# Fewer, larger transfers around the attention of a hybrid encoder layer, and a third bank for the maxima

## The chip, the cores and the metric

The kernel runs on one core of a Trainium2 chip. A core has five engines that work side by side, each with its own queue of instructions: TensorE (PE, with its weight loads as PEld), VectorE (DVE), ScalarE (ACT), GpSimd (POOL) and SyncE (SP), which here issues nearly all transfers. Sixteen DMA engines move the data between the chip's memory (DRAM tiles and tensors) and the on-chip buffers. TensorE writes its products into PSUM, eight banks of 512 fp32 columns for 128 partitions. The metric is the device time of one launch in microseconds.

## The reference

One layer for two groups of requests that share weights: a prompt of 2048 frames, and 8 sample streams of 16 new frames each with 1024 cached ones. Each goes through a combined input projection, then in parallel a causal depthwise convolution and an attention with a learned forgetting bias, then an output projection and a gated feed-forward network. What matters here is the attention:

```
def _attend(q, k, v, cum_q, cum_k, q_pos, k_pos):
    s = jnp.einsum('bqhd,bkhd->bhqk', q, k, preferred_element_type=jnp.float32) * (HEAD_DIM ** -0.5)
    s = s + (cum_q[..., :, None] - cum_k[..., None, :])
    mask = k_pos[None, :] <= q_pos[:, None]
    s = jnp.where(mask, s, NEG_INF)
    p = jax.nn.softmax(s, axis=-1)
    return jnp.einsum('bhqk,bkhd->bqhd', p.astype(v.dtype), v)
```

There are 8 heads of 64 channels; `cum` is the running sum of the log forget values of a head. All data are fp32.

## The kernel before

**Stages.** The trace shows them in this order: the projections of the gated inputs, values and forget values (to about 340 us), those of queries and keys (to about 600 us), the attention (to about 1190 us), the output projection (to about 1400 us), and the feed-forward network (to the end). Only the attention and what feeds it are touched.

**The prompt's attention.** Heads go in 4 pairs p, queries in 4 blocks qb of 512; a step is one (p, qb) of `STEPS`, 16 in all. A softmax needs each query's maximum before the scores can be exponentiated with keys on the partitions, so the scores are made twice. `score_maxima` makes them with queries on the partitions, in pieces of 512 keys: one product `mx` (L952), for the diagonal a mask product (L956), and a VectorE reduction into `M` (L957). A step has 8(qb+1) pieces, 8, 16, 24 or 32. After a step the maxima `Z` are transposed into `pz` (L968), copied to `mrow` (L970) and sent to the row `AUX` of the operand `Q2` of that step (L972), where they enter the second making of the scores as one more row of the contraction. `attend` makes these: `s` from two products (L1035 with `K1` and `Q1`, L1041 with `K2` and `Q2`) and a mask product on the diagonal (L1043), the exponential `e` on ScalarE (L1045), the products with the values `pv` (L999), and the sums of `e` by products with ones (L988) and by additions on GpSimd (L1011) and VectorE. Pieces run ahead of the scores: 32 at first (`AHEAD`), later up to 42 by an order written in `attend`.

**The end of a step.** `end_of_step` copies the unnormalised output to `zc`, the sums to `sm` (rows 0, 32, 64, 96), and sends them row by row to `sum_d` (L1080). Some units of work later, by a list of due times, `load` brings them back on 128 partitions (L1084), `invert` adds and inverts them and sends them to `inv_d` (L1090), `back` spreads each head's inverses over 64 partitions of `R` (L1094), and `divide` multiplies (L1097) and stores.

**The background.** `background` is woven between the scores: first the norm of the convolution, then the sample streams. `sample_setup` makes the forgetting bias of all streams and heads and sends it to `bias_d` (four quarters of keys) and `biasn_d` (new keys). `next_bias` loads a stream's bias into `S`, two streams ahead: 8 transfers for four quarters and two heads (L1218), 2 for the new keys (L1222). `sample_scores` adds products to it (lane matmuls, all under the helper's line L1105), `sample_values` takes the softmax and the values. Keys `kc` (L1208) and values `vc` (L1234) of a stream come as two transfers of 1 MB each, with 3 and 2 buffers.

**Order and banks.** The tile framework's planner fixes each engine's order when the kernel is built; some orders are forced by hand (`after`, `late`). The banks are shared out by name: `BANKS = {"u": 3, "cv": 2, "tr": 2, "ss": 1}`. In the attention `u` holds the scores `s`, `cv` the pieces `mx` and the transposes `pz`, `tr` the outputs and sums, `ss` the background's lanes.

Of the kernel before, what the change touches and what calls it, by code (L numbers as in the profile page):

```python
# [6 lines left out]
F32 = mybir.dt.float32  # L7
# [4 lines left out]
ALU = mybir.AluOpType  # L12
# [4 lines left out]
P = 128  # L17
# [3 lines left out]
NTP = T // P  # L21
NT = NTP + 1
TT = NT * P
NS = 8
QS = 16
H = 8
HD = 64
NP = H // 2
PAST = 1024
# [17 lines left out]
AHEAD = 32  # L47
# [11 lines left out]
AUX = 96  # L59


def f32(ap):
    return ap.bitcast(F32)
# [64 lines left out]
class Layer:  # L128
# [30 lines left out]
    def run(self, stop=99):  # L159
        tc = self.tc  # L160
        self.pinned = self.last_load = None
        self.LZ = ExitStack()
        with ExitStack() as ctx:
            d = self.dram = ctx.enter_context(tc.tile_pool(name="dram", bufs=1, space=DRAM))
            self.keep = ctx.enter_context(self.pool(name="keep", bufs=1))
            self.LB = ExitStack()
            self.big = self.LB.enter_context(self.pool(name="big", bufs=16, side="right"))
            self.ps = ctx.enter_context(self.pool(name="ps", bufs=1, space=PSUM))
            self.h_d = d.tile([P, CB, 2, TT], F32, name="h_d")
            self.u_d = d.tile([P, 4, HIST + T], F32, name="u_d")  # L170
            self.y_d = d.tile([P, 4, TT], F32, name="y_d")
            self.q_d = d.tile([H, P, T], F32, name="q_d")
            self.k_d = d.tile([H, P + 2, T], F32, name="k_d")
            self.cat_d = d.tile([P, CB, TT], F32, name="cat_d")
            self.x1_d = d.tile([P, CB, TT], F32, name="x1_d")
            self.ht_d = d.tile([P, 3, 7, 4, NW], F32, name="ht_d")
            self.r_d = d.tile([len(HALVES), P, NW], F32, name="r_d")
            self.gt_d = d.tile([P, 3, 7, NF // 2, NW], F32, name="gt_d")
            self.sup_d = d.tile([NF, 4, P, 512], F32, name="sup_d")
            self.sdn_d = d.tile([3, 4, 4, P, 512], F32, name="sdn_d")  # L180
            self.bias_d = d.tile([4, NS * H, PAST // 4], F32, name="bias_d")
            self.biasn_d = d.tile([NS * H, QS], F32, name="biasn_d")
            self.qs_d = d.tile([P, NP, P], F32, name="qs_d")
            self.sum_d = d.tile([NP, 4, 4, 512], F32, name="sum_d")
            self.inv_d = d.tile([NP, 4, 2, 512], F32, name="inv_d")
            self.open_input()
            self.load_constants()
            with ExitStack() as c1:
                self.project_u_v(c1)
            if stop > 1:  # L190
                self.project_q_k()
            if stop > 2:
                with ExitStack() as c2:
                    self.attention(c2)
                self.out_projection(stop)
                return
            else:
                while self.todo:
                    self.parts(9, TT)
                self.conv_part(999, TT)  # L200
            for st in (self.LZ, self.LC, self.RS, self.R, self.L, self.LB):
                st.close()
# [728 lines left out]
    def score_maxima(self):  # L931

        nc = self.nc
        self.mx, self.nscore, self.last_product = [], 0, None
        spread = None
        for n, (p, qb) in enumerate(STEPS):
            if qb == 0:
                self.loading = self.keys(p)
            self.kv[p] = next(self.loading)
            K2 = self.kv[p][1]  # L940
            Q2, Z, M = self.Q2[n % 4], self.Z[n % 2], self.M[n % 2]
            if n < 2:
                nc.gpsimd.memset(Z, 0.0)
            t = slice(qb * 512, qb * 512 + 512)
            nc.sync.dma_start(f32(Q2[0:HD]), self.q_d[2 * p:2 * p + 2, 0:HD, t].rearrange("h r t -> r h t"))
            for i in range(8):
                h, j = i // 4, i % 4
                for kb in range(qb + 1):
                    diag = kb == qb
                    w = (j + 1) * P if diag else 512  # L950
                    mx = self.bank("cv", "mx")
                    self.mx.append(nc.tensor.matmul(mx[:, :w], Q2[0:AUX, h, j * P:(j + 1) * P], K2[kb][0:AUX, h, :w], start=True, stop=not diag))  # L952
                    if self.last_product:
                        self.after(self.mx[-1], self.last_product)
                    if diag:
                        nc.tensor.matmul(mx[:, w - P:w], self.masks[:, 2], self.masks[:, 0], start=False, stop=True)  # L956
                    self.last_max = nc.vector.tensor_reduce(M[:, i, kb:kb + 1], mx[:, :w], AX.X, ALU.max)  # L957
                    if spread and i * (qb + 1) + kb == 3:
                        self.spread_maxima(*spread)
                    yield 0  # L960
            nc.vector.tensor_reduce(Z[:, AUX:AUX + 8], M[:, :, 0:qb + 1], AX.X, ALU.max)
            spread = (Z, Q2)
        self.spread_maxima(*spread)

    def spread_maxima(self, Z, Q2):
        nc, r = self.nc, slice(AUX, AUX + 8)
        pz = self.bank("cv", "pz", (P, P))
        nc.tensor.transpose(pz, Z, self.ident)  # L968
        m = self.lp.tile([P, P], F32R, tag="mrow", name="mrow", bufs=1)
        nc.vector.tensor_copy(m[r], pz[r])  # L970
        for i in range(8):
            nc.sync.dma_start(f32(Q2[AUX:AUX + 1, i // 4, i % 4 * P:(i % 4 + 1) * P]), f32(m[AUX + i:AUX + i + 1]))  # L972

    def attend(self, p, qb, n):

# [86 lines left out]
    def end_of_step(self, p, qb, zc, sums):  # L1062


        nc, wk = self.nc, self.awk
        parts = 2 if qb else 1
        r = slice(0, 64 * parts)
        sm = wk.tile([P, 512], F32, tag="sm", name="sm", bufs=1)
        self.last_exp = nc.scalar.copy(sm[r], sums[r])
        cat = self.cat_d[:, 4 + p, qb * 512:(qb + 1) * 512]  # L1070
        R = wk.tile([P, 512], F32, tag="R", name="aR", bufs=1)
        if (p, qb) == STEPS[-1]:
            spread = self.bank("ss", "R")
# [2 lines left out]
            nc.vector.tensor_tensor(zc, zc, R, ALU.mult)  # L1076
            nc.gpsimd.dma_start(cat, zc)
            return
        for i in range(2 * parts):
            nc.sync.dma_start(self.sum_d[p, qb, i:i + 1], sm[32 * i:32 * i + 1])  # L1080
        w = wk.tile([P, 2, 2, 4], F32, tag="inv", name="inv")

        def load():
# [6 lines left out]
            nc.sync.dma_start(self.inv_d[p, qb].rearrange("h (a c) -> a h c", c=4), w[:, 0])  # L1090

        def back():
            for h in range(2):
                nc.sync.dma_start(R[HD * h:HD * h + HD], self.inv_d[p, qb, h:h + 1].broadcast_to([HD, 512]))  # L1094

        def divide():
            self.after(nc.vector.tensor_tensor(zc, zc, R, ALU.mult), self.last_max)  # L1097
# [37 lines left out]
    def sample_setup(self, bank):  # L1135

        nc, a, sm = self.nc, self.a, self.smp
# [9 lines left out]
        sel = sm.tile([P, NS + QS], F32, name="sel")  # L1147
# [14 lines left out]
        for h in range(2):  # L1162
            o = slice(HD * h, HD * h + HD)
# [12 lines left out]
        for b in range(2):  # L1176
            pb = bank.rearrange("p (i k) -> p i k", i=4)
            for i in range(4):
# [4 lines left out]
                suf[:n, 4 * b:4 * b + 4].unsqueeze(2).broadcast_to([n, 4, P]), ALU.add)  # L1183
            yield
        lm = sm.tile([P, NS, H], F32, name="lm")
        nc.vector.tensor_tensor(lm, self.logf[:, NTP, :].unsqueeze(1).broadcast_to([P, NS, H]),
                                sel[:, 0:NS].unsqueeze(2).broadcast_to([P, NS, H]), ALU.mult)
        yield
        pn = bank[:, :QS]
        self.pe(pn[:n, :], lm.rearrange("p s h -> p (s h)"), sel[:, NS:], start=True, stop=True)  # L1190
# [20 lines left out]
    def next_bias(self, b):  # L1211

        if b < NS:
            S = self.smp.tile([P, PAST + NP * QS], F32, tag="S", name="S", bufs=2)
            for j in range(4):
                for h in range(2):
                    rows = self.bias_d[j].rearrange("(s g h) k -> s h g k", s=NS, h=2)[b, h]
                    self.nc.sync.dma_start(S[32 * j + QS * h:32 * j + QS * h + QS, :PAST].rearrange("p (g k) -> p g k", g=NP),  # L1218
                                           rows.unsqueeze(0).broadcast_to([QS, NP, PAST // 4]))
            for h in range(2):  # L1220
                rows = self.biasn_d.rearrange("(s g h) k -> s h g k", s=NS, h=2)[b, h]
                self.nc.sync.dma_start(S[QS * h:QS * h + QS, PAST:].rearrange("p (g k) -> p g k", g=NP),  # L1222
                                       rows.unsqueeze(0).broadcast_to([QS, NP, QS]))
            kS = self.smp.tile([P, NP, QS], F32, tag="kS", name="kS", bufs=2)
            self.nc.sync.dma_start(kS, self.a["o_k"][:, :, T + b * QS:T + (b + 1) * QS].rearrange("g p t -> p g t"))
            self.S.append((S, kS))
# [559 lines left out]
def host_layout(inp):  # L1786
    import numpy as np

    inp = {n: np.asarray(v) for n, v in inp.items()}

    def c(x):
        return np.ascontiguousarray(x)
# [5 lines left out]
    def cols(w):  # L1798
# [21 lines left out]
        "w_down": c(inp["w_down"][0].reshape(NF // 2, 2, P, CB, P).transpose(1, 3, 2, 0, 4)),  # L1820
        "kcT": c(inp["cache_k"][0].reshape(NS, PAST, NP, P).transpose(0, 3, 2, 1)),
        "vc": c(inp["cache_v"][0].reshape(NS, PAST, DC)),
        "clfT": c(inp["cache_logf"][0].reshape(NS, 8, P, H).transpose(2, 1, 0, 3).reshape(P, 8, NS * H)),
        "ident": np.eye(P, dtype=np.float32),
    }
    i = np.arange(P)
# [8 lines left out]
    g = i % 32 // 8  # L1835
# [39 lines left out]
```

## Time and profile before

| | us |
|---|---|
| median of 3 runs (2797.84 to 2798.93) | 2798.88 |
| the profiled execution by its own time | 2804.1 |
| its span, first to last instruction | 2802.3 |
| PE busy in the span | 2716.7 (97%) |
| DVE busy | 2029.7 (72%) |
| ACT busy | 1235.4 (44%) |
| share of the 16 DMA engines in use by the hardware queue | 67.0% |

How to read the profile: all durations come from the one profiled execution. The times of windows and timelines count from the span's start. In a timeline row the number in brackets is the time that the engine stood idle before the instruction, with the instruction or transfer that ended the wait. A row of a group of instructions ends with its busy time, the mean duration of one, and the idle time before them. "PEclk" is TensorE's granted clock as a share of full speed. A SyncE row such as `SPq L972 DMA_DIRECT2D Q<-mrow x8` is eight issues of transfers from tile `mrow` to tile `Q`; its duration is the time of the issuing, not of the transfers.

### The profile page before, as it was taken

How to read it: one execution, taken by the hardware profiler on the slowest of the kernel's cores; microseconds unless marked ns; L12 is line 12 of the kernel's file. 1: busy time of each engine (PE TensorE's matmuls, PEld its weight loads, DVE VectorE, ACT ScalarE, POOL GpSimd, SP SyncE). 2: the span in 40 equal slices, each digit the busy share in tenths (PEclk: the TensorE clock that was granted, in tenths of full speed). 3: DMA queues.
4: the chain of work that ended last, by engine and by line, in shares of the span. 5: the costliest groups of instructions: out<-in, count | busy, mean ns of one | idle time of the engine just before them, and what ended most of it. 6: DMA issues, size and time to landing. Idle time of an engine off the chain costs nothing.

```text
span 2802.3 us, 49088 instructions
## 1 busy us (share of the span) xinstructions
PE 2716.7 (97%) x16930; PEld 2397.9 (86%) x16930; DVE 2029.7 (72%) x4132; ACT 1235.4 (44%) x2472; POOL 500.6 (18%) x686
## 2 busy tenths in 40 slices
PE   7999999999999989999999999999999999999999
PEld 6899988874445545498999999999999999999999
DVE  2798898974656566545397989877887778776765
ACT  4543323343444333444354446444554446555552
POOL 3454411223443221314201120000000000000000
PEclk9999999989999999999999999999999999999999
DMA  8863567673436577265576869866786769787873
GB/s 320 255 193 107 177 225 260 207 199 97 131 105 179 160 223 240 62 218 189 172 264 204 303 205 314 275 213 215 243 285 208 227 194 319 248 284 252 278 248 116
DMA packets 416978, 603.55 MB, mean 215 GB/s; under 512 B 65141, under 2 KB 280341, under 8 KB 414681
## 3 DMA queue, kind: packets, MB, share of 16 engines
q1 hardware_dynamic: 416520, 600.05, 67.0%
q8 instruction: 133, 2.18, 0.3%
q14 instruction: 117, 0.95, 0.1%
q0 software_dynamic: 208, 0.37, 0.0%
HBM read 426.00 MB, written 174.25 MB: 214 GB/s over the span
## 4 chain that ended last, share of the span: by engine, by line
PE 82%; DMA 8%; DVE 5%; issue 2%; ACT 1%; POOL 1%; SPq 1%; DVEq 0%; ACTq 0%; POOLq 0%
PE z L1665 45%; PE z L524 6%; PE acc L1353 5%; PE pv L999 4%; PE mx L952 3%; PE pa L332 3%; PE pvv L352 3%; PE pg L332 3%; PE s L1035 2%; PE lane L1105 2%; PE s L1041 2%; PE sm L988 1%; DMA wraw<-w_in 1%; DVE rW L1370 1%; DMA kc<-kcT 1%
## 5 line engine op out<-in xcount | busy, mean ns | idle before, releaser
L1665 PE MATMUL z<-rT,rW 128*128 128x360 f32 (+1 forms) x8316 | 1384.4, 328 | 3.9 <-ACT rW L1369 1.4
L1665 PEld LDWEIGHTS z<-rT,rW 128*128 128x128 f32 x8316 | 1380.1, 188 | 6.3 <-ACT rW L1369 2.4
L1369 ACT ACTIVATE rW<-rR 128x512 fp32r<-128x512 f32 x714 | 434.7, 616 | 388.7 <-PE z L1665 277.0
L1370 DVE TENSOR_TENSOR rW<-rR,rW 128x512 fp32r<-128x512 f32 x714 | 477.3, 673 | 160.3 <-ACT rW L1369 155.8
L712 DVE SCALAR_TENSOR_TENSOR cv<-cu,cpar,cv 128x384 f32<-128x384 f32 x580 | 311.7, 615 | 2.5 <-ACT cv L710 2.4
L1045 ACT ACTIVATE e<-s 128x512 f32<-128x512 f32 (+3 forms) x320 | 166.4, 532 | 284.2 <-PE s L1041 163.9
L957 DVE TENSOR_REDUCE M<-mx 128x1 f32<-128x512 f32 (+2 forms) x320 | 190.2, 605 | 133.7 <-PE mx L952 106.4
L524 PE MATMUL z<-hqx,wqh 128*128 128x384 f32 (+1 forms) x768 | 197.4, 333 | 1.3 <-DVE logf L359 1.3
L1369 ACT ACTIVATE rT<-traw 128x360 fp32r<-128x360 f32 (+1 forms) x315 | 149.8, 501 | 81.8 <-DMA traw<-gt_d 50.8
L1370 DVE TENSOR_TENSOR rT<-traw,rT 128x360 fp32r<-128x360 f32 (+1 forms) x315 | 158.0, 531 | 34.0 <-ACT rT L1369 33.3
L952 PE MATMUL mx<-K,Q 96*128 96x512 f32 (+2 forms) x320 | 142.4, 458 | 21.1 <-DVE M L957 12.6
L999 PE MATMUL pv<-e,V 128*64 128x512 f32 (+3 forms) x640 | 157.1, 558 | 0.0
L952 PEld LDWEIGHTS mx<-K,Q 96*128 96x128 f32 x320 | 62.8, 199 | 109.9 <-DVE M L957 57.2
L524 PEld LDWEIGHTS z<-hqx,wqh 128*128 128x128 f32 x768 | 136.1, 188 | 17.6 <-issue 12.4
L1353 PE MATMUL acc<-ch,woh 128*128 128x360 f32 (+1 forms) x384 | 127.1, 333 | 6.3 <-DVE xo L1361 3.9
L1593 DVE TENSOR_TENSOR rR<-rR 128x512 f32<-128x512 f32 (+1 forms) x136 | 92.0, 696 | 56.6 <-DMA rR<-w_down 50.5
L1035 PE MATMUL s<-Q,K 128*128 128x512 f32 (+3 forms) x320 | 131.0, 409 | 0.3 <-ACT e L1045 0.2
L1353 PE MATMUL acc<-ch,wol 128*128 128x360 f32 (+1 forms) x384 | 126.7, 330 | 0.0
L524 PE MATMUL z<-hqx,wql 128*128 128x384 f32 (+1 forms) x384 | 126.5, 329 | 0.0
L1041 PE MATMUL s<-Q,K 128*128 128x512 f32 (+3 forms) x320 | 120.3, 376 | 4.6 <-DMA Q<-mrow 4.6
L1353 PE MATMUL acc<-cl,woh 128*128 128x360 f32 (+1 forms) x384 | 122.9, 330 | 0.7 <-DVE cl L1370 0.6
L1011 POOL TENSOR_TENSOR sums<-e,sums 128x512 f32<-128x512 f32 x72 | 97.4, 1353 | 100.2 <-ACT e L1045 96.9
(317 smaller groups left out, 3728.5 us busy)
## 6 DMA issues: line engine op xcount, KB each, us to landing
rR<-sup_d SPq DMA_DIRECT2D x176, 256.0 KB
rR<-w_gate SPq DMA_DIRECT2D x132, 256.0 KB
traw<-gt_d SPq DMA_DIRECT2D x154, 180.0 KB
rR<-w_down SPq DMA_DIRECT2D x104, 256.0 KB
rR<-sdn_d SPq DMA_DIRECT2D x96, 256.0 KB
rR<-w_up SPq DMA_DIRECT2D x88, 256.0 KB
sup_d<-rR SPq DMA_DIRECT2D x88, 256.0 KB
wa<-w_ada SPq DMA_DIRECT2D x16, 1024.0 KB
```

The costliest lines, as they stand in the source:

```text
L332: nc.tensor.matmul(pz[:, :n], w[:, m], x[:, :n], start=(c == 0 and k == 0), stop=(c == CB - 1 and k == 2))
L524: nc.tensor.matmul(z[:, :n], w[:, m], x[:, :n], start=(c == 0 and k == 0), stop=(c == CB - 1 and k == 2))
L712: self.pin(nc.vector.scalar_tensor_tensor(dst, src, w, acc[i], ALU.mult, ALU.add))
L952: self.mx.append(nc.tensor.matmul(mx[:, :w], Q2[0:AUX, h, j * P:(j + 1) * P], K2[kb][0:AUX, h, :w], start=True, stop=not diag))
L957: self.last_max = nc.vector.tensor_reduce(M[:, i, kb:kb + 1], mx[:, :w], AX.X, ALU.max)
L999: product = nc.tensor.matmul(z[0][HD * h:HD * h + HD, off:], V[kt // 4][:, kt % 4, HD * h:HD * h + HD], es[h][:, off:], start=(kt == 0), s ...
L1035: first = nc.tensor.matmul(s[:, off:], K1[kb][:, h, sl], Q1[:, h, off:], start=True, stop=False)
L1041: self.last_s = nc.tensor.matmul(s[:, off:], K2[kb][:, h, sl], Q2[:, h, off:], start=False, stop=not diag)
L1353: self.nc.tensor.matmul(z[:, :n], w[:, m], y, start=(first and i == 0 and k == 0), stop=(last and i == len(terms) - 1 and k == 2))
L1369: copy = self.nc.scalar.activation(hi, raw, AF.Copy)
L1370: engine.tensor_tensor(lo, raw, f32(hi), ALU.subtract)
L1665: nc.tensor.matmul(z, W[:, x, m], t[:, y, :w], start=(k == 0 and i == 0), stop=(k == n - 1 and i == 2))
```

## The change

It does five things.

- Sums: a step's rows of `sm` go to `sum_d` in one transfer with a partition step of 32.
- Inverses: both heads go to `R` in one transfer, its source the two rows of `inv_d`, each repeated 64 times.
- Maxima: the eight rows of `mrow` go to a new DRAM tile `mrow_d` in one transfer; `take_maxima` brings them to the row of `Q2` in another, four pieces later.
- Bias: the rows of the forgetting bias are ordered stream, head of the pair, pair (before: stream, pair, head of the pair), from the host's layout of the cached forget values on. So a quarter of a stream's bias is one transfer, its source two rows of 4 KB, each repeated 16 times; the bias of the new keys is a fifth. The product `lm` is made in two halves for this order.
- Banks: from the 42nd piece of maxima on, each third is made in a bank of `u`.

```diff
+            self.mrow_d = d.tile([8, P], F32, name="mrow_d")
...
-                    mx = self.bank("cv", "mx")
+                    mx = self.bank("u" if len(self.mx) > AHEAD + 8 and len(self.mx) % 3 == 2 else "cv", "mx")
...
-                    if spread and i * (qb + 1) + kb == 3:
-                        self.spread_maxima(*spread)
+                    if spread and i * (qb + 1) + kb in (3, 7):
+                        (self.spread_maxima if i * (qb + 1) + kb == 3 else self.take_maxima)(*spread)
...
         self.spread_maxima(*spread)
+        self.take_maxima(*spread)
...
-        for i in range(8):
-            nc.sync.dma_start(f32(Q2[AUX:AUX + 1, i // 4, i % 4 * P:(i % 4 + 1) * P]), f32(m[AUX + i:AUX + i + 1]))
+        nc.sync.dma_start(self.mrow_d, f32(m[r]))
+
+    def take_maxima(self, Z, Q2):
+        self.nc.sync.dma_start(f32(Q2[AUX:AUX + 1]).rearrange("o h q -> o (h q)"), self.mrow_d.rearrange("(o r) c -> o (r c)", o=1))
...
-        for i in range(2 * parts):
-            nc.sync.dma_start(self.sum_d[p, qb, i:i + 1], sm[32 * i:32 * i + 1])
+        nc.sync.dma_start(self.sum_d[p, qb, 0:2 * parts], sm[0:64 * parts:32])
...
-            for h in range(2):
-                nc.sync.dma_start(R[HD * h:HD * h + HD], self.inv_d[p, qb, h:h + 1].broadcast_to([HD, 512]))
+            nc.sync.dma_start(R, self.inv_d[p, qb].unsqueeze(1).broadcast_to([2, HD, 512]))
...
-        nc.vector.tensor_tensor(lm, self.logf[:, NTP, :].unsqueeze(1).broadcast_to([P, NS, H]),
-                                sel[:, 0:NS].unsqueeze(2).broadcast_to([P, NS, H]), ALU.mult)
+        for h in range(2):
+            nc.vector.tensor_tensor(lm[:, :, NP * h:NP * h + NP], self.logf[:, NTP, h::2].unsqueeze(1).broadcast_to([P, NS, NP]),
+                                    sel[:, 0:NS].unsqueeze(2).broadcast_to([P, NS, NP]), ALU.mult)
...
-                for h in range(2):
-                    rows = self.bias_d[j].rearrange("(s g h) k -> s h g k", s=NS, h=2)[b, h]
-                    self.nc.sync.dma_start(S[32 * j + QS * h:32 * j + QS * h + QS, :PAST].rearrange("p (g k) -> p g k", g=NP),
-                                           rows.unsqueeze(0).broadcast_to([QS, NP, PAST // 4]))
-            for h in range(2):
-                rows = self.biasn_d.rearrange("(s g h) k -> s h g k", s=NS, h=2)[b, h]
-                self.nc.sync.dma_start(S[QS * h:QS * h + QS, PAST:].rearrange("p (g k) -> p g k", g=NP),
-                                       rows.unsqueeze(0).broadcast_to([QS, NP, QS]))
+                rows = self.bias_d[j].rearrange("(s h g) k -> s h (g k)", s=NS, h=2)[b]
+                self.nc.sync.dma_start(S[32 * j:32 * j + 32, :PAST], rows.unsqueeze(1).broadcast_to([2, QS, PAST]))
+            rows = self.biasn_d.rearrange("(s h g) k -> s h (g k)", s=NS, h=2)[b]
+            self.nc.sync.dma_start(S[:32, PAST:], rows.unsqueeze(1).broadcast_to([2, QS, NP * QS]))
...
-        "clfT": c(inp["cache_logf"][0].reshape(NS, 8, P, H).transpose(2, 1, 0, 3).reshape(P, 8, NS * H)),
+        "clfT": c(inp["cache_logf"][0].reshape(NS, 8, P, NP, 2).transpose(2, 1, 0, 4, 3).reshape(P, 8, NS * H)),
```

## The prediction

> **What bounds the kernel now.** I read the page's chain of work that ended last first, then the windows of the attention stage, then the timelines of TensorE, VectorE and SyncE around its gaps, and last the DMA view of short stretches.
>
> ```profile
> PE 82%; DMA 8%; DVE 5%; issue 2%; ACT 1%; POOL 1%; SPq 1%; DVEq 0%; ACTq 0%; POOLq 0%
> ```
> ```profile
> 640.00:930.00 290.00, 279.01 (x1402) 143.28 (x1400) 166.77 (x313) 124.77 (x272) 112.74 (x121) 0.98 0.45 129
> 930.00:1130.00 200.00, 182.73 (x1695) 100.92 (x1694) 128.82 (x315) 71.75 (x173) 37.31 (x33) 0.94 0.70 214
> 927.00:1127.00 200.00, 181.29 (x1678) 99.99 (x1674) 129.26 (x316) 70.93 (x172) 36.75 (x32) 0.94 0.69 209
> ```
>
> The columns are window, length, busy time of PE, PEld, DVE, ACT and POOL, granted clock, DMA share, GB/s. TensorE carries the kernel. The change lies in the attention, from about 600 to 1190 us. While the prompt's attention runs with the conv norm beside it (640 to 930) TensorE idles 11 us of 290 and the DMA engines are half free. From 930 to 1130, when the sample streams run as background, it idles 17.3 us of 200 and the DMA engines are 70% busy. The gaps of that stretch, from TensorE's and VectorE's timelines:
>
> ```profile
> 937.05 1.08 PE L1105 MATMUL lane<-kc,Qbd 128*32 128x128 f32 x16 [3.44 <-DVE S L1105]
> 990.06 0.77 PE L1041 MATMUL s<-Q,K 128*128 128x512 f32 x1 [4.62 <-DMA Q<-mrow]
> 1050.47 0.58 PE L952 MATMUL mx<-K,Q 96*128 96x256 f32 x1 [5.52 <-DVE rsx L1105]
> 1049.12 0.69 DVE L1097 TENSOR_TENSOR zc<-zc,aR 128x512 f32<-128x512 f32 x1 [7.09 <-DMA aR<-inv_d]
> 1050.00:1059.00 9.00, 8.53 (x33) 3.96 (x34) 4.27 (x11) 1.48 (x4) 0.40 (x1) 0.50 0.65 184
> ```
>
> So three late transfers (a stream's bias, the row of maxima, the spread inverses) make 13.6 of the 17.3 us, and after the longest gap the granted clock was 0.50 for 9 us, worth 4.3 us more. SyncE, which issues nearly every transfer, is a cause:
>
> ```profile
> 603.86 5.03 SPq L972 DMA_DIRECT2D Q<-mrow  x8
> 608.99 1.30 SPq L569 DMA_DIRECT2D k_d<-qp  x2
> 1025.98 11.47 SPq L972 DMA_DIRECT2D Q<-mrow  x8
> 1040.26 1.25 SPq L1094 DMA_DIRECT2D aR<-inv_d  x2
> 1043.64 8.44 SPq L1218 DMA_DIRECT2D S<-bias_d  x8
> ```
>
> Eight pieces of maxima hold its queue for 5.0 us when the rings are free and 11.5 us when they are full, and the spread inverses go out behind them.
>
> **On how many engines a transfer runs.** This decides the change, and the DMA view shows it: each engine that takes part ends with one closing packet of a few bytes, so the packets under 512 B count engines. First the stretch 759 to 767.7 us, then 675.5 to 678.4.
>
> ```profile
> DMA packets 831, 1.58 MB, mean 182 GB/s; under 512 B 59, under 2 KB 59, under 8 KB 831
> ...
> Q<-q_d SPq DMA_DIRECT2D x1, 512.0 KB
> K<-k_d SPq DMA_DIRECT2D x1, 512.0 KB
> K<-k_d SPq DMA_DIRECT2D x1, 264.0 KB
> Q<-q_d SPq DMA_DIRECT2D x1, 256.0 KB
> ```
> ```profile
> DMA packets 8, 0.01 MB, mean 3 GB/s; under 512 B 4, under 2 KB 4, under 8 KB 8
> ...
> sum_d<-sm SPq DMA_DIRECT2D x4, 2.0 KB
> ```
>
> Four transfers of 128, 128, 66 and 64 rows have 59 closing packets: 16+16+16+11. The one of 66 rows ran on 11 engines, the largest number up to 16 that divides 66. A single row ran on one engine: four transfers, four packets of 2 KB and four closing ones. So the outermost count of a transfer is dealt out in equal shares. In the diff the bias of a stream becomes `rows.unsqueeze(1).broadcast_to([2, QS, ...])` and the inverses `[2, HD, 512]`: the outermost count of the source is the two heads, where it was 16 and 64 rows before. I take it that they run on **two engines**, as the rows of 66 and of 1 speak for; the other end of the bound is 16, as the same bytes run now.
>
> The Trainium skill says the same of the number in "DMA: Bandwidth & Descriptors", section "Why a DMA increments its semaphore by 16 and not by 1" (the largest k up to 16 that divides the slowest dimension of both sides). The trace agrees for 66 rows and for 1. That section adds that on this queue these are always the lowest-numbered k engines, which no row here shows. By it both heads' shares fall on the same two engines every time; were the pair to change from one transfer to the next, each engine's load would stay near 0.69.
>
> **The change part by part.** Here is what moves from 927 to 1127 us, and what one engine does when busy.
>
> ```profile
> q1 hardware_dynamic: 35730, 41.54, 68.9%
> ...
> S<-bias_d SPq DMA_DIRECT2D x64, 64.0 KB
> ...
> aR<-inv_d SPq DMA_DIRECT2D x12, 128.0 KB
> ...
> S<-biasn_d SPq DMA_DIRECT2D x16, 4.0 KB
> ```
> ```profile
> q1 hardware_dynamic: 160, 0.26, 14.6%
> ...
> aR<-inv_d SPq DMA_DIRECT2D x2, 128.0 KB
> ```
> ```profile
> 1026.00:1030.00 4.00, 4.00 (x38) 2.31 (x37) 3.36 (x6) 1.20 (x2) 2.16 (x2) 1.00 1.03 393
> ```
>
> *One engine's rate.* Two transfers of inverses alone (667.5 to 673 us, 262,144 B at 14.6% of 16 engines for 5.5 us, 12.85 engine-us) give 20.4 B/ns. Ends: 393/(1.03 x 16) = 23.8 in a full stretch, 209/(0.689 x 16) = 19.0 over the 200 us. I take 20.4, the same kind of transfer.
>
> *Bias of the streams.* 64 x 64 KB and 16 x 4 KB are 4.26 MB; half of it on each of two engines is 2.13 MB, **104 us** (90 to 112).
> *Spread inverses.* 12 x 128 KB, six steps: 1.57 MB, half is 0.79 MB, **39 us** (33 to 41).
> *The rest on the same engines.* 68.9% of 200 us is 138; these two kinds had a sixteenth each, 5.83 MB/16/20.4 = 18. Left: **120 us**.
>
> Sum, if it is the same two engines each time, as I assume (the other bound, with the pair changing, is the 138 of now): 120 + 104 + 39 = **263 us of work in 200 us** (245 to 273): 63 too many (45 to 73). Every transfer of keys, values, queries and of the row of maxima that uses 16 engines ends with its share on those two, behind what was issued earlier. TensorE's order is fixed, so a late load stops the scores too. Before 927 us there is room: the inverses there add some 6 us of landing each to transfers that are rarely waited for, and I cost that at nothing, which fails where the division follows closely.
>
> What the end of the stretch gives back:
>
> ```profile
> 1124.38 2.00 SPq L1234 DMA_DIRECT2D vc<-vc  x2
> 1148.57 1.06 PE L1105 MATMUL lane<-vc,ST 128*32 128x128 f32 x26
> ```
>
> The last values are issued by 1126.4 and used at 1148.6: allow 2 us of issue and landing and about 20 us of slack are eaten first. 63 - 20 = +43.
>
> *Maxima: one write, one read.* Eight issues become two, so a step's 5.0 us (0.63 each) fall to about 1.3. On the stretch at 604 us the store of keys at 608.99 goes out some 4 us earlier: -4 (0 to -8). But the row now goes through memory and is fetched four pieces later. Where the queue is empty this hides; between 930 and 1140 both legs wait behind the two engines. Waiting for the write also holds SyncE, and behind it the keys, values and inverses: +6 by the 4.62 us gap above, once or twice (0 to +20).
>
> ```profile
> L1080 SPq DMA_DIRECT2D sum_d<-sm x52: 215/248/732, 646.3 to 1156.0; - x52
> L1105 DVE TENSOR_TENSOR S<-S,lane 128x256 f32<-128x256 f32 x32 | 13.2, 413 | 8.4 <-PE lane L1105 8.3
> ```
>
> *Sums:* four rows in one transfer save 37 of 52 issues of 0.25 us, off the chain: 0. *Order of the forget values, one more VectorE multiply:* 32 columns, at most the 0.41 us of the add over 256, once, beside the lanes: 0.
>
> *Each third piece of maxima in a bank of the scores.* What it can win and its risk:
>
> ```profile
> PE mx L952 <- DVE M L957: 12.6, 18, 2.0
> PE s L1035 <- ACT e L1045: 0.2, 1, 0.2
> ```
>
> Of 12.6 us that TensorE waits for a maximum to be reduced, about half lies after 640 us, where the change applies. The scores hardly wait for their three banks (0.2 us), so a fourth user of them is mostly free. I take -2 (-6 to +4).
>
> Sum: 63 - 20 - 4 + 6 - 2 = **+43 us**. The gaps of 13.6 us that exist now are inside the 200 us and so aren't taken off again. The profiled execution is 2804.1 us by its own time (span 2802.3) and would become 2847; the median of the runs is 5.2 lower, so 2798.88 + 43 = **2842 us**.
>
> **The rivals.**
> A, *the transfers stay spread* (all 16 engines, or another pair each time): then the change does what it says. SyncE is relieved of 96 issues of maxima, 40 of bias, 37 of sums and 15 of inverses. The gaps at 937, 990 and 1050 us go with the half clock behind the last: 13.6 + 4.3 = 18, so 2781 us. For it: the queue is plainly in the way at 1026. Against: the closing packets. The deciding point is the share on the two engines: below 200 us of work in 200 it wins. The Trainium skill speaks for this rival in the same page's section "Bandwidth": batch transfers, those under 64 KB are ruled by their descriptors. The bias here goes from 64 KB to 128 KB a transfer, and no run here shows that batching alone is worth anything. By that rule the sum would be A's.
>
> B, *the overload fits in the slack*: the engines run at 23.8 B/ns (+45), the slack takes 20, and A's gains of 18 and the 4 at the keys' store come off too: +3, 2802 us. Against: 2048 B packets took longer, not less, when the rings were full (19.0 above).
>
> C, *slower by the row of maxima alone*, with 16 engines for the rest: its two legs miss the first product that needs them in steps of 32 pieces. Four such steps at 4.62 us less half of A's 18 give +9, 2808 us.
>
> **How the numbers follow.** Two engines and overload: 0.75. A: 0.14. B: 0.05. C: 0.06. Runs of this kernel tell 0.2% from no change, 5.6 us. Faster 0.14, same 0.05, slower 0.75 + 0.06 = 0.81. Range: the upper end is 73 with no slack allowed and 13 for waits, 2885; the lower takes in B and C and most of the slack, 2800. A is left out.
>
> **What would show it.** In the DMA view of a short stretch with one bias transfer: two closing packets, not 16, and for the inverses two. Between 930 and 1170 us long TensorE gaps ended by `S`, `kc`, `aR` or `Q`, while the mean DMA share falls although the stage waits for transfers. SyncE's rows of L972 at one issue per step. The stage before 930 nearly as long as now. I am wrong if the bias shows 16 closing packets, if the share stays at 0.69 and the stretch shrinks, or if the late transfers are only the row of maxima.

## The result, and the profile after

| | before | after |
|---|---|---|
| median, us (4 runs each) | 2798.46 (2797.84 to 2798.93) | 2864.28 (2862.73 to 2869.84) |
| ratio, 95% interval | | 1.0239 (1.0221 to 1.0257) |
| span of the profiled execution, us | 2802.3 | 2863.0 |
| mean granted TensorE clock from 930 to 1130 us | 0.94 | 0.84 |

The change costs 66 us. In the new program the lines have shifted by some: the maxima are L953, the scores L1039 and L1045, the write of the maxima L973 and their fetch L976, the spread inverses L1096, a stream's bias L1220 and L1222.

First the page's shares of the chain that ended last, then two windows of the kernel after (window, length, busy time of PE, PEld, DVE, ACT and POOL, granted clock, DMA share, GB/s):

```profile
PE 77%; DMA 12%; DVE 4%; issue 3%; POOL 1%; SPq 1%; ACT 1%; POOLq 0%; DVEq 0%; ACTq 0%
```
```profile
640.00:930.00 290.00, 279.01 (x1407) 145.05 (x1406) 171.15 (x312) 124.88 (x272) 116.30 (x119) 0.97 0.42 121
930.00:1130.00 200.00, 147.40 (x1216) 81.83 (x1216) 100.58 (x242) 58.16 (x138) 33.51 (x25) 0.84 0.54 157
```

Transfers rose from 8% to 12% of the chain. Before 930 us TensorE is as busy as it was. From 930 to 1130 it was busy for 182.7 us and is now busy for 147.4, and yet the DMA engines do less: their share fell from 0.70 to 0.54. So the stage waits for transfers while most engines stand still: the work is dealt out unevenly. TensorE's gaps of over 8 us from 930 to 1250, from its timeline:

```profile
946.45 1.08 PE L1107 MATMUL lane<-kc,Qbd 128*32 128x128 f32 x16 [8.57 <-DVE S L1107]
964.08 0.79 PE L953 MATMUL mx<-K,Q 96*128 96x512 f32 x1 [8.15 <-DVE M L958]
1036.14 0.44 PE L953 MATMUL mx<-K,Q 96*128 96x128 f32 x1 [17.89 <-DMA K<-k_d]
1120.87 0.80 PE L1039 MATMUL s<-Q,K 128*128 128x512 f32 x1 [8.77 <-DVE M L958]
1156.67 1.97 PE L1003 MATMUL pv<-e,V 128*64 128x512 f32 x4 [8.32 <-ACT zc L1024]
1195.57 1.08 PE L1107 MATMUL lane<-kc,Qbd 128*32 128x128 f32 x16 [11.21 <-DVE S L1107]
```

They add up to 62.9 us.

**Two engines.** From 670.5 to 678.7 us the DMA view of the kernel after holds one transfer of spread inverses and one of four sums:

```profile
DMA packets 138, 0.27 MB, mean 33 GB/s; under 512 B 6, under 2 KB 6, under 8 KB 138
...
q1 hardware_dynamic: 138, 0.27, 9.5%
...
aR<-inv_d SPq DMA_DIRECT2D x1, 256.0 KB
sum_d<-sm SPq DMA_DIRECT2D x1, 8.0 KB
```

132 packets of 2 KB carry the 264 KB. Six are closing packets: four for the four rows of sums, if those are dealt out like the rows of 66 and of 1, which leaves **two for 128 rows of inverses**. From 936 to 945 us only transfers of bias are moving:

```profile
DMA packets 121, 0.47 MB, mean 52 GB/s; under 512 B 6, under 2 KB 6, under 8 KB 121
...
q1 hardware_dynamic: 121, 0.47, 12.7%
```

115 packets of 4 KB are 3.6 transfers of 128 KB, so three end in these 9 us, with six closing packets: two each. The next view, 931 to 951 us, has the first bias of two streams behind one another:

```profile
DMA  5000012021111111111111111111111111111111
GB/s 15 1 1 1 2 13 26 1 29 59 57 49 49 49 57 57 49 49 49 57 57 49 49 57 57 49 49 49 48 51 57 57 49 49 49 57 57 49 49 49
...
q1 hardware_dynamic: 1277, 0.86, 13.1%
...
S<-bias_d SPq DMA_DIRECT2D x8, 128.0 KB
aR<-inv_d SPq DMA_DIRECT2D x1, 256.0 KB
```

Nine large transfers are under way and the digits stand at 1: one tenth of 16 engines, some 50 GB/s, and 13.1% of 16 is 2.1 engines. Had each transfer a pair of its own, nine of them would have kept far more than two engines busy. So it is the **same two engines** each time. SyncE, whose queue feeds them, is held by its issues (the prediction's full rings):

```profile
935.20 7.69 SPq L1220 DMA_DIRECT2D S<-bias_d  x4
942.94 0.58 SPq L1222 DMA_DIRECT2D S<-biasn_d  x1
943.56 2.15 SPq L1096 DMA_DIRECT2D aR<-inv_d  x1
946.04 7.13 SPq L1093 DMA_DIRECT2D inv_d<-inv  x1
```

The issue of 4 KB of inverses (L1093) took 7.13 us, when it takes about 0.4 in a quiet stretch (0.38 at 667.67 us). Counted over the trace from the starts and durations of the hardware queue's packets: between 927 and 1250 us exactly two packets are under way for 90.3 us (before, 927 to 1186: 6.1), and none for 52.0 us (73.1). Of the 52.0, 35.4 fall after 1190 us, when the last bias has landed; from 927 to 1190 it is 16.6 us of 263.

**What waits.** The transfers of spread inverses in the chain that ended last in the stretch from 930 to 1250 us (start, length, what):

```profile
943.56 19.28 DMA aR<-inv_d
...
964.03 8.66 DMA aR<-inv_d
...
1156.18 9.13 DMA aR<-inv_d
...
1184.44 10.24 DMA aR<-inv_d
...
1217.09 8.93 DMA aR<-inv_d
```

The chain of the kernel before, from 926 to 1186 us, has one:

```profile
1040.86 8.16 DMA aR<-inv_d
```

And that of the version with bias and inverses by head (its run is below), from 917 to 1170 us, has two:

```profile
929.41 2.87 DMA aR<-inv_d
...
1104.42 3.07 DMA aR<-inv_d
```

The five of the kernel after add up to 56.2 us, the two of the version by heads to 5.9, and the first of the five takes 19.28 us, behind eight bias transfers. Single transfers of prompt keys, queries and inverses (`inv_d`) of 9 to 12 us stand in both chains (11.45, 12.33 and 9.38 us after; 10.51, 12.12 and 10.66 by heads), so they don't tell the two apart. What hangs on the spread inverses is seen in the waits of the kernel after, 930 to 1250 us (total, times, longest):

```profile
DVE zc L1099 <- DMA aR<-inv_d: 40.8, 5, 13.5
...
ACT zc L1024 <- DMA cat_d<-zc: 22.5, 2, 12.2
...
PE lane L1107 <- DVE S L1107: 21.0, 3, 11.2
...
PE pv L1003 <- ACT zc L1024: 8.3, 1, 8.3
```

VectorE has one order for all its work. The division `zc` that waits for the inverses holds the reductions `M` and the additions to `S` behind it, and TensorE waits for those: this is the gap at 964 us, which names `M`, just after the division in the row below, and the gap at 1195.57 us, after a division at 1194.70 that waited 13.55 us. The gap at 1120.87 comes one step earlier in that work, from the sums on their way back, for which VectorE waited 9.63 us until 1119.45; the one at 946.45 waits for the bias itself. And the divided `zc` leaves its buffer late, so ScalarE can't copy the next one, and the products `pv` of the next step have no bank. From VectorE's timeline:

```profile
962.87 0.69 DVE L1099 TENSOR_TENSOR zc<-zc,aR 128x512 f32<-128x512 f32 x1 [13.53 <-DMA aR<-inv_d]
```

### The profile page after: what moved, and what is told of

Same layout as the page of the kernel before. It is cut to its first block, busy times and chain, and to the rows that moved or that the text cites. A ratio compares the mean times of both kernels' runs of the same rounds, so it can differ in the third digit from the quotient of the medians.

```text
span 2863.0 us, 48834 instructions
## 1 busy us (share of the span) xinstructions
PE 2718.8 (95%) x16930; PEld 2400.8 (84%) x16930; DVE 2034.9 (71%) x4133; ACT 1232.7 (43%) x2472; POOL 508.9 (18%) x686
## 4 chain that ended last, share of the span: by engine, by line
PE 77%; DMA 12%; DVE 4%; issue 3%; POOL 1%; SPq 1%; ACT 1%; POOLq 0%; DVEq 0%; ACTq 0%
PE z L1664 43%; PE z L525 6%; PE acc L1352 4%; PE pv L1003 4%; PE pa L333 3%; PE pvv L353 3%; PE mx L953 3%; PE pg L333 3%; PE lane L1107 2%; DMA aR<-inv_d 2%; PE s L1039 2%; PE s L1045 2%; DMA Q<-q_d 1%; PE sm L992 1%; DMA inv_d<-inv 1%
## 5 line engine op out<-in xcount | busy, mean ns | idle before, releaser
L953 PEld LDWEIGHTS mx<-K,Q 96*128 96x128 f32 x320 | 63.1, 207 | 137.8 <-issue 58.6
L953 PE MATMUL mx<-K,Q 96*128 96x512 f32 (+2 forms) x320 | 136.6, 467 | 43.0 <-DMA K<-k_d 18.6
L1039 PE MATMUL s<-Q,K 128*128 128x512 f32 (+3 forms) x320 | 137.3, 429 | 15.1 <-DVE M L958 9.2
L1045 PE MATMUL s<-Q,K 128*128 128x512 f32 (+3 forms) x320 | 121.9, 381 | 0.0
```

Source lines behind the costliest of these rows:

```text
L1039: first = nc.tensor.matmul(s[:, off:], K1[kb][:, h, sl], Q1[:, h, off:], start=True, stop=False)
L1045: self.last_s = nc.tensor.matmul(s[:, off:], K2[kb][:, h, sl], Q2[:, h, off:], start=False, stop=not diag)
```

## The experiments

Ratios are to the kernel before as run beside each; an interval stands behind each. Times in the text are medians.

**Bias by head.** The changed kernel, only the bias again in one transfer per head; its source is 16 repeats of one row.

```diff
-                self.nc.sync.dma_start(S[32 * j:32 * j + 32, :PAST], rows.unsqueeze(1).broadcast_to([2, QS, PAST]))
+                for h in range(2):
+                    self.nc.sync.dma_start(S[32 * j + QS * h:32 * j + QS * h + QS, :PAST], rows[h:h + 1].broadcast_to([QS, PAST]))
```

> The changed kernel, only the streams' bias again one transfer per head (16 rows each; 10 issues per stream in place of 5). Theory (two engines): by the prediction's terms the two engines then have 120 + 39 + 13 = 172 us of work in 200, so nothing overflows: 2800 to 2815 us, and a stretch with bias alone shows 16 closing packets per transfer. Rival (the row of maxima through memory and the held SyncE cause the loss): 2858 to 2870 us, since neither is touched. Rival (the inverses are the cause): within 5 us of 2864.

Measured: 2811.35 us, 1.0054 (1.003 to 1.0079). 53 us of the 66 are gone, with nothing done to the row of maxima. The first bias of the two streams now moves at a DMA share of 41.7% (926 to 936 us), where the kernel after had 13.1%.

**Inverses by head.** The same for the spread inverses alone.

```diff
-            nc.sync.dma_start(R, self.inv_d[p, qb].unsqueeze(1).broadcast_to([2, HD, 512]))
+            for h in range(2):
+                nc.sync.dma_start(R[HD * h:HD * h + HD], self.inv_d[p, qb, h:h + 1].broadcast_to([HD, 512]))
```

> The changed kernel, only the spread inverses again one transfer per head (64 rows each). Theory: 120 + 104 + 5 = 229 us of work on two engines in 200, still too many: 2820 to 2850 us, a part of the loss stays and VectorE's divisions no longer wait long for aR. Rival (bias alone is the cause): 2860 to 2866. Rival (inverses alone): 2798 to 2806.

Measured: 2835.57 us, 1.0143 (1.0115 to 1.0171). Both parts count. VectorE's waits for `aR` did not vanish, though: from 640 to 1250 us there are still 19.1 us in three waits, since spread inverses have shares on the two engines too, behind the bias.

**Both by head.** Maxima, sums and the third bank stay changed.

> The changed kernel with bias and inverses both one transfer per head: maxima, sums and banks stay changed. Theory (two engines carry the loss): no worse than the kernel before, 2785 to 2803 us. Rival (the maxima through memory or the bank of the scores carry it): 2830 us or more.

Measured: 2792.52 us, 0.9982 (0.997 to 0.9995). The whole loss, 72 us to this version, is in the merged broadcasts of bias and inverses. The same work is compared in the next rows: cut at the starts of the 21st, the 181st and the last product with `K1` and `Q1`, first this version, then the kernel after, then the kernel before.

```profile
653.00:917.00 264.00, 255.89 (x1319) 133.96 (x1318) 162.35 (x296) 116.62 (x257) 114.06 (x116) 0.99 0.43 125
917.00:1170.00 253.00, 232.04 (x2022) 125.60 (x2022) 160.77 (x365) 97.99 (x230) 55.67 (x47) 0.95 0.59 180
```
```profile
660.00:930.00 270.00, 259.01 (x1320) 134.92 (x1316) 161.74 (x297) 116.93 (x258) 112.47 (x116) 0.97 0.42 122
930.00:1248.00 318.00, 240.56 (x2021) 129.24 (x2022) 155.09 (x364) 97.63 (x230) 59.28 (x47) 0.85 0.49 143
```
```profile
654.00:926.00 272.00, 262.54 (x1322) 134.64 (x1321) 157.88 (x295) 117.56 (x257) 107.76 (x116) 0.97 0.43 124
926.00:1185.00 259.00, 240.25 (x2032) 128.26 (x2032) 162.67 (x374) 98.64 (x232) 56.17 (x47) 0.95 0.58 176
```

The stretch with the streams takes 318 us in place of 253: 65 more. TensorE's idle time is 77.4 in place of 21.0, which is 56.4, and the same products, some 2021, keep it busy for 240.6 in place of 232.0, 8.5 more. The clock is 0.85 in place of 0.95, but that it makes the 8.5 is not shown: the kernel before needs 240.25 at a clock of 0.95. The stage before takes 270 in place of 264, 6 more, and 272 in the kernel before. In these two executions the kernel after also starts the work 7 us later, before its first merged transfer (670.8 us), and takes 6 us less behind it; no run explains these two.

**Bias by columns.** As many issues as by heads, but each still with both heads.

```diff
+                for c in range(2):
+                    k = slice(PAST // 2 * c, PAST // 2 * c + PAST // 2)
+                    self.nc.sync.dma_start(S[32 * j:32 * j + 32, k], rows[:, k].unsqueeze(1).broadcast_to([2, QS, PAST // 2]))
```

> The changed kernel, each bias transfer cut in two by columns: as many issues as the run by heads, the same bytes, but the outermost count of each source is still the two heads. Theory (count of the outermost dimension decides): 2860 to 2872 us, no gain. Rival (the size or number of the transfers decides): the time of the run by heads, 2800 to 2815 us.

Measured: 2862.35 us, 1.0227 (1.0201 to 1.0252). Same issues and same bytes as by heads, and 51 us slower: the outermost count decides, not the number or size of the transfers.

**Half of the bias.** Two quarters of keys by head, two and the new keys as changed.

> The changed kernel with two of the four quarters of each stream's bias one transfer per head and two as changed. This is a dose between 2811 us (all by head) and 2864 us (none). By the prediction's own form (overload less 20 us of slack) the two engines have 120 + 52 + 6 + 39 = 217 us of work in 200, which the slack swallows: 2808 to 2816 us. Rival form (each transfer on two engines costs its own stall, wherever it stands): half of the difference, 2832 to 2844 us.

Measured: 2833.2 us, 1.0127 (1.0107 to 1.0148): 22 of the 53 us for half of the dose. The form "overload less slack" of the prediction expected at most 2816 and falls; the range of the rival, that each transfer on the two engines costs time where it stands, holds.

**Bias from ScalarE's queue.** Only the engine that issues differs.

```diff
-                self.nc.sync.dma_start(S[32 * j:32 * j + 32, :PAST], ...
+                self.nc.scalar.dma_start(S[32 * j:32 * j + 32, :PAST], ...
```

> The changed kernel with the merged bias transfers issued by ScalarE's queue in place of SyncE's; bytes, counts and engines as changed. Theory A (the two engines' backlog itself makes the later loads late, since each 16-engine transfer has a share on them): 2845 to 2875 us. Theory B (what costs is that SyncE is held behind rings that are full, and the keys and inverses are issued late): 2795 to 2820 us. In between, both have a part. ScalarE's exponentials then wait behind up to 10 issues of 0.6 us at the start, some 3 us against either.

Measured: 2859.03 us, 1.0209 (1.0189 to 1.0229). SyncE no longer issues the bias, and nearly all of the loss stays. Its waits, 930 to 1250 us:

```profile
DVE zc L1099 <- DMA aR<-inv_d: 28.9, 6, 10.3
...
ACT e L1049 <- DMA S<-bias_d: 24.5, 3, 14.3
DVE S L1107 <- DMA S<-biasn_d: 21.9, 4, 11.7
```

Now ScalarE's exponentials wait in its queue. VectorE still waits 28.9 us for the inverses (40.8 in the kernel after) and 21.9 for the bias of the new keys (12.1). So the loss doesn't need a held SyncE; the backlog of the two engines makes nearly all of it from another queue too. How much of the remaining loss comes from ScalarE being held in SyncE's place was not separated.

The next five take the rest of the change apart, with the transfers spread.

**Maxima direct.** The version by heads with the eight pieces of maxima sent straight to the operand again.

> The run with bias and inverses by head (2792.5 us), and the row of maxima again sent straight to the operand in eight pieces. By the prediction the maxima's two legs and the earlier store of keys cancel to +2, so without them 2790 us (2785 to 2797). Rival (the relief of SyncE at 604 us and in the stretch is what this version wins): 2796 to 2802 us.

Measured: 2795.8 us, 0.9994 (0.9978 to 1.001), against 0.9982: by the medians the two-leg row is worth some 3 us here, but the two intervals overlap, so that is not shown.

**Sums by row.** The version by heads with four issues per step for the sums again.

> The run with bias and inverses by head (2792.5 us), and the sums again row by row, 37 issues more. By the prediction 0: 2790 to 2795 us. Rival (SyncE's queue is what matters): 2796 us or more.

Measured: 2792.9 us, 0.9987 (0.9972 to 1.0002). Nothing.

**Banks back.** The version by heads with all maxima in their own two banks.

```diff
-                    mx = self.bank("u" if len(self.mx) > AHEAD + 8 and len(self.mx) % 3 == 2 else "cv", "mx")
+                    mx = self.bank("cv", "mx")
```

> The run with bias and inverses by head (2792.5 us), and all pieces of maxima again in their own two banks. By the prediction the third bank is worth 2 us: 2794 to 2797 us, and the time that TensorE waits for a maximum to be reduced grows. Rival (the bank disturbs the scores): below 2791 us.

Measured: 2782.84 us, 0.9948 (0.9932 to 0.9963). Without the third bank it is 10 us faster. The number is the rival's, its reason is not: the scores' waits for a bank are much the same (3.0 and 1.9 us in the two traces).

**The order of the bias rows alone**, on the kernel before, still by head.

> The kernel before with only the order of the bias rows changed (stream, head, pair), still one transfer per head: rows of 4 KB in place of four of 1 KB, and lm in two halves; maxima, sums, inverses and banks as before. The prediction priced this at 0: 2794 to 2801 us. Rival (the rows of 4 KB are what the version with the banks back, 2782.8 us, owes most of its 14 us to): 2782 to 2790 us.

Measured: 2802.09 us, 1.0001 (0.9988 to 1.0013). Rows of 4 KB in place of four of 1 KB are worth nothing.

**The third bank alone**, on the kernel before.

> The kernel before with only the third bank for the maxima. The prediction: -2, 2794 to 2798 us. Rival (from the run with the banks back, 9.7 us below its pair): the third bank lets the maxima run ahead to operands that have not landed, 2803 to 2812 us. If it comes out within 3 us of the kernel before, the 9.7 us belong to the order that the planner chose in that pair and not to the bank as such.

Measured: 2796.22 us, 0.9984 (0.9971 to 0.9997), as the prediction had it. Alone the bank wins 4 us; together with the maxima through memory it loses 10. TensorE's waits between 640 and 1190 us in four kernels, in the order before, bank alone, both by head, banks back:

```profile
PE mx L952 <- DVE M L957: 9.4, 12, 1.4
...
PE mx L952 <- DMA Q<-q_d: 2.0, 1, 2.0
```
```profile
PE s L1035 <- DMA Q<-q_d: 8.5, 1, 8.5
PE mx L952 <- DMA Q<-q_d: 8.0, 3, 2.8
...
PE mx L952 <- DVE M L957: 1.8, 4, 0.8
```
```profile
PE mx L953 <- DMA Q<-q_d: 12.6, 3, 6.5
...
PE mx L953 <- DVE M L958: 1.0, 2, 0.6
```
```profile
PE mx L953 <- DVE M L958: 5.8, 11, 1.1
...
PE mx L953 <- DMA Q<-q_d: 1.0, 2, 0.7
```

With the third bank the maxima no longer wait for a reduction (9.4 to 1.8, 5.8 to 1.0), run ahead, and meet queries that have not landed (2.0 to 16.5 with the scores', 1.0 to 12.6). That is the give and take. Why it nets to a gain in one pair and a loss in the other stays open: the planner also orders the whole attention anew when a bank changes, and no run holds that order fixed.

**Maxima through memory alone**, with banks, sums, inverses as before and the bias by head in the new row order.

> The kernel before with the new row order of the bias (worth nothing by the run before) and the maxima through memory in two transfers; sums row by row, inverses and bias by head, banks as before. With the sums merged as well this was 0.9948 of the kernel before. If the relief of SyncE by 96 issues of maxima wins that (the rival in the prediction that says the transfers stay spread and the queue is relieved): 0.993 to 0.997 of the kernel before. If the maxima win nothing without the merged sums (37 issues), or the planner's order is what differs: 0.999 to 1.003.

Measured: 2779.14 us, 0.9931 (0.9915 to 0.9947); its six runs lie between 2778.28 and 2790.74, the profiled one at the upper end, so no row of it is read here. This and the version with the banks back beat both kernels. The latter's windows show what there was to win from 930 to 1130 us:

```profile
930.00:1130.00 200.00, 195.60 (x1857) 108.18 (x1854) 140.54 (x339) 83.00 (x201) 42.06 (x37) 1.00 0.68 217
```

TensorE is busy for 195.6 us of 200 (before 182.7), at the full clock all the way, with nearly the same DMA share as before (0.68, 0.70).

## Why the prediction held, and where it did not

The time, 2864.28 us, is 22 above the 2842 forecast and inside the range. By the prediction's steps:

- **Two engines per merged transfer: right**, by the closing packets. That the pair is always the same was an assumption there; the DMA share of 13.1% with nine transfers under way shows it. The rule of the Trainium skill in "DMA: Bandwidth & Descriptors", section "Why a DMA increments its semaphore by 16 and not by 1", agrees with both, and with four closing packets for four rows of sums. That the pair is the lowest-numbered, no row shows.
- **One engine's rate, 20.4 B/ns: near for the inverses, too low for the bias.** The inverses above moved 270,336 B in 9.5% of 16 engines for 8.2 us, 12.5 engine-us: 21.7. The bias moved 115 packets of 4 KB in 12.7% of 16 engines for 9 us, 18.3 engine-us: 25.8. So 39 becomes 36, and 104 becomes 83. With the 120 for the rest, which was not measured again, the work of the two engines is 239 and not 263, an overload of 39 us in place of 63.
- **63 - 20 = +43: this is the step that failed.** The two merged transfers cost 72 us, 65 in the stretch and 6 ahead of it. The sum took the two engines for a pipe that overflows, and a reserve of 20 us at the end that fills first. The pipe was nearly full: from 927 to 1190 us the hardware queue is empty for 16.6 us of 263. But the overload is not the price. Estimated at the measured rates it would be none with the bias by head (120 + 36 and 10 for the spread bias, 166 us of work in 200), 2 with half of it, 8 with the inverses by head and 39 in the kernel after; over the version by heads these lost 19, 41, 43 and 72 us by their medians. Each is 19 to 39 more. The runs show in its place the waits of a chain (sums, inverses, `aR`, `zc`, then VectorE's next reduction and the next `pv`), in which every late transfer is a step: the spread inverses alone hold 56.2 us of it, where the version by heads has 5.9. How the 72 us divide between the two was not separated.

And the reserve did not fill. The last stream's values are issued once the products with those of the stream before are made, here those at 1202.68 (in the kernel before at 1123.24, its issue at 1124.38):

```profile
1202.68 1.95 PE L1107 MATMUL lane<-vc,ST 128*32 128x128 f32 x64
```
```profile
1203.82 1.25 SPq L1233 DMA_DIRECT2D vc<-vc  x2
```
```profile
1227.94 3.10 PE L1107 MATMUL lane<-vc,ST 128*32 128x128 f32 x64 [3.03 <-DVE ST L1107]
```

From the end of their issue to their use are 22.9 us, as in the kernel before (1126.4 to 1148.6, 22.2): the slack moved along with the delay and paid for nothing. The use waited for VectorE's `ST`, not for the values. That the forecast came within 22 us of the time is in part luck: the low rate of the bias added 24 us. With the measured rates the same sum gives some 2818 us.

- **The stage before 927 us at nothing: right against the kernel before** (270 us, where that has 272), but not because the inverses cost nothing there: the version by heads needs 264, so they cost 6 us that the rest of the change had won.
- **Maxima by memory, +6 - 4 = +2: wrong in sign.** With the old banks they win: 0.9931 against 1.0001 with the row order alone, some 19 us. With the third bank it is 3 us by the medians, inside the intervals. The feared wait for the row is in no list of TensorE's waits of the kernel after, and the 4.62 us that the kernel before lost there are gone. What this term is worth inside the changed kernel itself was not tried.
- **Third bank, -2: right alone** (-4), wrong beside the maxima by memory (+10), as above.
- **Sums and row order at 0: right** (0.9987 against 0.9982; 1.0001).
- **Rival A (the transfers stay spread, 2781 us)** fell as a forecast, since they don't. Its price was wrong for this change too: with bias and inverses spread and all else changed it is 2792.52. Only without the third bank do two versions come to its time, 2779.14 and 2782.84. SyncE relieved of 96 issues of maxima is the likely source of that, but the planner's order can change with them, and no run holds it fixed. The rule of the Trainium skill's section "Bandwidth" of the same page, to batch transfers, did not decide here: bias from 64 to 128 KB a transfer lost 53 us, and cut by columns into 64 KB again it kept 51 of them. **Rival B (it fits in the slack)** fell, although its rate of 23.8 was nearer to the bias's 25.8: the slack it counted on was not there. (The 19.0 held against it is a mean over packets of all sizes; those of 2048 B alone ran at 20.6 from 927 to 1127 us.) **Rival C (the row of maxima is what costs)** fell with the run by heads, 2792.52 us.
- **What would show it:** two closing packets for bias and for inverses, long gaps behind `S` and behind the inverses, a DMA share that falls while the stage waits, and one issue of maxima per step all came. The longest gap, 17.89 us, was behind the prompt's keys, which the list had not.

## What to carry to other kernels

Before transfers are merged, look at the outermost count on both sides of the new one: a source that repeats two rows ran here on two engines, however many rows it filled, and everything that used all 16 then ended behind them. Merge where the outermost count stays large, or where many small transfers fill the queue, as the pieces of maxima probably did. And price a slowed transfer by the chain that hangs on it, step by step: here neither the bandwidth left over on the other engines nor the slack at the end paid for it. Before a slack is counted, look at what releases the transfer: if that is late as well, the slack only moves.

## What the runs showed of the hardware that was not expected

- Moving the bias to ScalarE's queue hardly helped (2859.03 against 2864.28 us): the transfers stayed on the engines that they share, and ScalarE's exponentials now waited in the queue.
- One engine moved 25.8 B/ns in packets of 4 KB and 21.7 in packets of 2 KB, both from repeated rows in DRAM.
- One issue of a 4 KB transfer held SyncE for 7.13 us behind such a backlog.
- With the gaps the granted clock fell too: its mean in the stretch was 0.85 in place of 0.95. What that cost was not separated.
